# Reordering the projections of a one-core MLA + NSA transformer block: where the second projection and the branch values stand, which queue stores, and who makes low parts

## The chip, the cores and the metric

The kernel runs on one core of a Trainium2 chip. The metric is the device time of one execution in microseconds (us), taken as the median of several. The core has a matrix engine (PE), a vector engine (DVE), a scalar engine (ACT), GpSimd (POOL) and SyncE (SP); the last two issue transfers on DMA queues of their own. Each engine runs its own instructions strictly in the order written for it and waits on semaphores for the others.

## The reference

The block has a width of 1024, a sequence of 1024 tokens and one layer, and all in float32:

```python
h = h + token_mixer(rmsnorm(h, attn_norm), w_in, ...)
h = h + conv_ffn(h, ffn_norm, w_up, conv_w, conv_b, w_down)
return rmsnorm(h, final_norm)

def token_mixer(n, w_in, ...):
    z = n @ w_in        # c_q 384, c_kv 256, k_rope 32, q 512, six k/v of 128, 24 gates
    o_mla = mla_attention(c_q, c_kv, k_rope, ...)
    o_nsa = nsa_attention(q_n, k_c, v_c, k_s, v_s, k_w, v_w, gates, ...)
    return concatenate([o_mla, o_nsa], -1) @ w_o
```

`mla_attention` norms `c_q` and `c_kv`, projects them a second time (`rmsnorm(c_q) @ w_uq` gives the queries of 8 heads, `rmsnorm(c_kv) @ w_ukv` the keys and values), rotates the rope parts and does causal softmax attention. `nsa_attention` has 8 heads over 2 groups and three branches: a compressed one (`k_c`, `v_c` pass a small MLP by blocks of 32 tokens), a selected one (the top 16 of 16 blocks, so all causal keys) and a window of 512. Their outputs are summed under sigmoid gates. `conv_ffn` is a gated FFN of 2816 channels with a causal convolution of width 3.

## The kernel before, in words

**Precision.** A float32 operand is split into a high part (a rounded copy, made by ACT) and a low part (the operand minus its high part, made by DVE or POOL). A product takes three matmuls: high by high, high by low and low by high (`mm3`). A tile of a *Dense* item is 128 output channels by 1024 tokens, in a PSUM buffer `A` of two banks (there are two such buffers), with 8 steps over the input channels of 6 matmuls each. DVE then evacuates it in two instructions that also scale (`evac_scaled`, L212), and buffer `A` is free again.

**Stages.** In the profile of before: until 50 us the first three input tiles are computed while `x` streams in, with the norm of `x`. From 50 to about 206 us come the items of `run_items`: window keys (`kw`), gates and rope keys (`gr`), three tiles of `c_q`, four NSA query tiles (`q_tile`, stored to DRAM as `qnd`), the branch values (`Values`: 8 tiles of 128 tokens by 256 channels, 24 matmuls of 256 columns each, in PSUM buffer `B`, evacuated by ACT into `vsw`), and two tiles of `c_kv`. The second projection follows (206 to 266 us): six query tiles (`proj("q")`, 18 matmuls each; four of nope rows and two of rope rows, which `rotate` turns), then four key tiles (`proj("kv")`, 12 matmuls), each with two `mla_value` tiles behind it (6 matmuls each, buffer `B`, evacuated by ACT at L562). Each query or key tile is split (`split_rows`: high on ACT L428, low on DVE or POOL L429) and stored to DRAM as `qd` and `kd` (L568, L573). Then `attend(plan)` runs NSA query tiles 2 to 7, MLA pairs and the two short NSA tiles; the output projection, the FFN and the last norm come after it.

**What attention starts with.** NSA tile 2 takes its queries back from `qnd` (`fetch`, L727), splits them into `qs` (`prep`, L738 and L739), and multiplies them with `kd[j, g]`: the selected and window keys, loaded back from `kswd` into a doubled layout and split (`dup`, L591). Products go to PSUM buffer `A` (L629). DVE adds a mask (`dsel`, `dwin`) while taking a minimum (`soften`, L637), ACT takes the exponential (L640), PE transposes (L651), and PE multiplies by `vsw` (L666). The compressed branch goes its own way at the start of each NSA tile: PE L744 into `B`, DVE L746 and L749, POOL L750 and L751, ACT L755 (exponential), DVE L756.

**What sets the order.** The program is written as one sequence; each engine gets its instructions in that order, apart from local moves that a scheduler makes. `later(n, fn)` holds a step back until `tick()` has been called n times (after each step of a Dense item, for example). Transfers are issued by SP (`load`, `move`) or by POOL (`side`), in the order of that queue. Buffers come from rings: 37 of one size (`big`), 4 (`wide`), 3 for weights that are loaded (`w`). A buffer that is taken again makes its new writer wait for the last reader of the old content, a store included.

Of the kernel before, what the change touches and what calls it, by code (L numbers as in the profile page):

```python
# [17 lines left out]
P = 128  # L18
# [26 lines left out]
WARM = 8  # L45
FIRST = 1
RC, RR = (6, 0), (6, 2)
# [3 lines left out]
def body(ctx: ExitStack, tc: tile.TileContext, io, out):  # L51
# [57 lines left out]

    def split_g(x, g):  # L110

        hi, lo = big(list(x.shape), F32R, "hi"), big(list(x.shape), F32R, "lo")
# [117 lines left out]
    rs_x = big([P, T], name="rsx")  # L230
    first_w = [{} for _ in range(3)]


# [25 lines left out]
    def x_tile(k, s):  # L259
        n = s.stop - s.start  # L260
        x = big([P, n], name="x")
        in_turn(load, x, io["xT"][k * P:(k + 1) * P, s])

        def parts():
            h, l = split_g(x, col(C_AN + k))
# [62 lines left out]
    class Dense:  # L328
# [5 lines left out]
        def prep(self):  # L334
            self.w = split(load_w(self.ap, [P, KD, self.mw]), new=wide)

# [9 lines left out]
    def run_items(items, ahead=2):  # L346
        for j in range(min(ahead, len(items))):
            items[j].prep()
        for j, it in enumerate(items):
            it.run()  # L350
            if j + ahead < len(items):
                items[j + ahead].prep()

# [6 lines left out]
    def compress(src, pos0, w1n, w2n, put, t0):  # L360
        st = {}

        def gather():
            st["w1"] = [load_w(io[w1n][:, 8 * j:8 * j + 8], [P, 8, P]) for j in range(2)]
            st["w2"] = half([P, 64], name="w2")
# [50 lines left out]
    def rotate(t, n):  # L416

        w = big([P, T], name="sw")
        dve.stream_shuffle(out=w[:n], in_=t[:n], mask=[(j + 16) % 32 for j in range(32)])
        for c in range(2):  # L420
            s = slice(c * 512, (c + 1) * 512)
            pool.tensor_tensor(out=t[:n, s], in0=t[:n, s], in1=rope[0][c][:n], op=OP.mult)
            dve.tensor_tensor(out=w[:n, s], in0=w[:n, s], in1=rope[1][c][:n], op=OP.mult)
            pool.tensor_tensor(out=t[:n, s], in0=t[:n, s], in1=w[:n, s], op=OP.add)

    def split_rows(t, n, le="dve", new=wide):
        h, l = new([P, T], F32R, "hi"), new([P, T], F32R, "lo")
        act(h[:n], t[:n], AF.Copy)  # L428
        (dve if le == "dve" else pool).tensor_tensor(out=l[:n], in0=t[:n], in1=f(h)[:n], op=OP.subtract)  # L429
        return h, l  # L430

    def done_kw(o):
        t = evac_scaled(o, 1.0, rs_x)
        move(ksw_d[1], t)

    def done_gr(o):
# [16 lines left out]
        def rope_put():  # L453
            for j, t in enumerate(split_rows(kr, 32)):
                move(kr_d[j], f(t)[0:32])

        later(4, rope_k)

    lat = {n: dict(t=[], acc=big([P, T], name="acc"), rs=big([P, T], name="rs" + n)) for n in ("q", "kv")}

    def latent(n, m0, count, rank, gain):
        def done(o):
            L = lat[n]
            t = evac_scaled(o, 1.0, rs_x, name="c" + n)
            L["t"].append(t)
            sumsq(L["acc"], t, len(L["t"]) == 1)
            i = len(L["t"]) - 1
# [6 lines left out]
            if len(L["t"]) == count:  # L474
                later(6, lambda: L.update(rc=rms_cols([L["acc"]], rank)))
                later(9, lambda: rms_rows(L["rs"], L["rc"]))

        return [Dense(io["w_in"][m0 + i], done) for i in range(count)]

    def q_tile(r):  # L480
        def done(o):
            move(qn_d[:, r], evac_scaled(o, col(C_QS + r), rs_x))

        return Dense(io["w_in"][M_QN + r], done)

    vsw = [big([P, 4, 256], name="vsw") for _ in range(2)]

    class Values:


        def prep(self):
            self.w = [split(load_w(io["w_v"][:, 4 * j:4 * j + 4], [P, 4, 256])) for j in range(2)]

# [15 lines left out]
    def weights(n, ap, kt, w):  # L509
        def go(k):  # L510
            wts.setdefault(n, []).append(split(load_w(ap[k * P:(k + 1) * P], [P, w])))
        return [lambda k=k: go(k) for k in range(kt)]

    items = [Dense(io["w_in"][M_KW], done_kw), Dense(io["w_gr"], done_gr, 64)]
    items += latent("q", M_CQ, 3, RANK_Q, C_QN)
    items += [q_tile(r) for r in range(4)] + [Values()]
    items += latent("kv", M_CKV, 2, RANK_KV, C_KVN)
    for j, fn in enumerate(weights("q", io["w_uq"], 3, 768)):
        later(100 + 2 * j, fn)

# [12 lines left out]
    dist = {}  # L533
    later(50, masks)
    later(75, mask_sel)
    run_items(items)


# [11 lines left out]

    vm = [big([P, 2, 512], name="v") for _ in range(4)]

# [11 lines left out]

    def put_rows(t, dst, m, le, new=wide):
        for j, t in enumerate(split_rows(t, P, le, new)):
            for a in range(2):
                move(dst[2 * m + a, j, 0:64, :], f(t)[64 * a:64 * a + 64])  # L568

    def put_rope(t, m):  # L570
        for j, t in enumerate(split_rows(t, P)):
            for a in range(4):
                move(q_d[4 * m + a, j, 64:96, :], f(t)[32 * a:32 * a + 32])  # L573

    for j, fn in enumerate(weights("kv", io["w_ukv"], 2, 1024)):
        later(4 + 3 * j, fn)
    for m in range(4):
        t = proj("q", m, -MLA_SCALE)
        later(1, lambda t=t, m=m: put_rows(t, q_d, m, "pool" if m % 2 else "dve"))
    for m in range(2):  # L580
        t = proj("q", 4 + m, -MLA_SCALE)
        later(2, lambda t=t: rotate(t, P))
        later(9, lambda t=t, m=m: put_rope(t, m))

# [3 lines left out]
    def dup(j, g):  # L588
        t = sb.tile([P, T], F32, name=nm("kw"), tag="w", bufs=NW)
        for q in range(2):  # L590
            load(t[64 * q:64 * q + 64], ksw_d[j][64 * g:64 * g + 64])  # L591
        kd[j, g] = split(t)

    for j in range(2):
        for g in range(2):
            later(1 + 3 * g + 10 * j, lambda j=j, g=g: dup(j, g))

# [123 lines left out]
    def nsa_tile(i):  # L721
# [71 lines left out]
        def unit(br, rp):  # L793
            j = br - 1
            kb, d, v0 = (0, dist["sel"], 0) if br == 1 else (max(0, i - 4), dist["win"], 128)
            n = (i + 1 - kb) * P
            rows = []
            for g in range(2):
                for r in (2 * rp, 2 * rp + 1):
# [4 lines left out]

                    rows.append(dict(passes=passes, n=n, d=d[:, d.shape[1] - n:], scale=SLOPES[h], total=None, h=h))

# [9 lines left out]
            def totals():  # L816
                for row in rows:
                    c = 8 * br + row["h"]
                    row["total"] = st["tot"][:, c:c + 1]

            return u, [(-1, totals)]
# [137 lines left out]
    for m in range(4):  # L959
# [618 lines left out]
```

## Time and profile before

| | |
|---|---|
| time, median of 3 runs | 1411.15 us (1410.7 to 1412.43) |
| the profiled execution's own time | 1415.98 us |
| its span in the trace | 1414.2 us, 18969 instructions |
| mean granted TensorE clock | 0.981 |
| stages of the part that is changed | 0 to 50 first tiles; 50 to 206 first projection; 206 to 266 second projection; attention from there |

The page gives the busy share of each engine over the span and in 40 slices of 35.4 us. The slices that matter here are the first eight. A view of waits tells for an engine how long it stood still, at which of its lines, and which instruction of another engine ended that; in the timeline the same stands in brackets behind the instruction that waited. Times of matmuls overlap, so the distance from one start to the next is the pace.

### The profile page before, as it was taken

How to read it: one execution, taken by the hardware profiler on the slowest of the kernel's cores; microseconds unless marked ns; L12 is line 12 of the kernel's file. 1: busy time of each engine (PE TensorE's matmuls, PEld its weight loads, DVE VectorE, ACT ScalarE, POOL GpSimd, SP SyncE). 2: the span in 40 equal slices, each digit the busy share in tenths (PEclk: the TensorE clock that was granted, in tenths of full speed). 3: DMA queues.
4: the chain of work that ended last, by engine and by line, in shares of the span. 5: the costliest groups of instructions: out<-in, count | busy, mean ns of one | idle time of the engine just before them, and what ended most of it. 6: DMA issues, size and time to landing. Idle time of an engine off the chain costs nothing.

```text
span 1414.2 us, 18969 instructions
## 1 busy us (share of the span) xinstructions
PE 1354.6 (96%) x6996; PEld 1092.5 (77%) x6996; DVE 1016.3 (72%) x1587; ACT 669.6 (47%) x1213; POOL 469.3 (33%) x347
## 2 busy tenths in 40 slices
PE   8999999599999999999998999999999999999995
PEld 7788987467887767877877778888888888888785
DVE  6463017677776766685598997787787877998796
ACT  6022122576765656673345554444444445354371
POOL 4246525414333434420000025556665551000100
PEclk9999999799999999999999999999999999999998
DMA  6131314811112117643651131222212237754543
GB/s 223 60 128 60 116 45 127 219 46 42 39 50 79 42 50 188 193 150 129 225 192 53 65 119 70 75 90 89 82 67 75 90 126 245 278 184 135 155 135 120
DMA packets 69117, 164.58 MB, mean 116 GB/s; under 512 B 9288, under 2 KB 22744, under 8 KB 69024
## 3 DMA queue, kind: packets, MB, share of 16 engines
q1 hardware_dynamic: 60768, 145.53, 31.5%
q0 software_dynamic: 5376, 13.24, 3.3%
q10 hardware_dynamic: 2880, 4.60, 0.9%
q8 instruction: 55, 0.90, 0.3%
q14 instruction: 38, 0.31, 0.1%
HBM read 126.25 MB, written 37.09 MB: 115 GB/s over the span
## 4 chain that ended last, share of the span: by engine, by line
PE 54%; DVE 25%; ACT 7%; issue 5%; POOL 4%; DMA 3%; SPq 1%; DVEq 0%; ACTq 0%; POOLq 0%
PE A L629 6%; DVE wp L96 6%; PE O L666 6%; PE B L651 5%; PE A L204 4%; PE A L205 4%; PE A L207 4%; PE B L977 3%; PE B L979 3%; PE B L978 3%; PE A L977 3%; PE A L979 3%; PE A L978 3%; ACT hc L1051 3%; DVE hg L1163 3%
## 5 line engine op out<-in xcount | busy, mean ns | idle before, releaser
L640 ACT ACTIVATE p<-p,low 128x640 f32<-128x640 f32 (+7 forms) x192 | 142.6, 744 | 50.9 <-DVE low L637 47.3
L977 PE MATMUL B<-hi,wp 128*128 128x512 f32 x340 | 132.7, 390 | 0.9 <-DVE hg L1163 0.9
L978 PE MATMUL B<-lo,wp 128*128 128x512 f32 x340 | 132.6, 390 | 0.0
L98 POOL TENSOR_TENSOR wp<-w,wp 128x512 fp32r<-128x512 f32 x34 | 56.3, 1655 | 229.7 <-ACT wp L1112 229.7
L979 PE MATMUL B<-hi,wp 128*128 128x512 f32 x340 | 132.2, 389 | 0.0
L651 PE MATMUL B<-ident,p 128*128 128x128 f32 x816 | 123.1, 276 | 4.3 <-ACT pt L606 1.6
L651 PEld LDWEIGHTS B<-ident,p 128*128 128x128 f32 x816 | 96.7, 141 | 22.6 <-issue 6.2
L1112 ACT ACTIVATE wp<-ws 128x512 fp32r<-128x512 f32 x88 | 53.6, 628 | 99.8 <-DVE ws L1106 64.6
L96 DVE TENSOR_TENSOR wp<-ws,wp 128x512 fp32r<-128x512 f32 x54 | 66.9, 1243 | 44.6 <-ACT wp L1112 44.6
L204 PE MATMUL A<-hi,hi 128*128 128x512 f32 (+1 forms) x228 | 90.5, 397 | 1.0 <-DVE z L212 1.0
L205 PE MATMUL A<-lo,hi 128*128 128x512 f32 (+1 forms) x228 | 89.5, 393 | 0.0
L609 DVE COPY pt<-B 128x512 f32<-128x512 f32 (+3 forms) x154 | 77.5, 510 | 16.0 <-PE B L651 15.0
L606 ACT ACTIVATE pt<-B 128x512 f32<-128x512 f32 (+3 forms) x134 | 64.2, 481 | 50.6 <-PE B L651 50.2
L1051 ACT ACTIVATE hc<-hg,prm 128x1024 f32<-128x1024 f32 x44 | 54.5, 1243 | 66.3 <-DVE hg L1163 66.3
L104 ACT ACTIVATE hi<-w 128x1024 fp32r<-128x1024 f32 (+2 forms) x34 | 34.4, 1022 | 100.1 <-PE A L205 60.0
L1053 DVE SCALAR_TENSOR_TENSOR hc<-hg,prm,hc 128x1022 f32<-128x1022 f32 x44 | 78.1, 1776 | 0.6
L629 PE MATMUL A<-hi,qs 128*128 128x320 f32 (+5 forms) x192 | 64.8, 390 | 14.0 <-DVE pr L212 10.1
L977 PE MATMUL A<-nh,wp 128*128 128x512 f32 x188 | 74.4, 396 | 3.7 <-ACT q L1143 3.7
L666 PE MATMUL O<-pt,vsw 128*64 128x256 f32 x528 | 76.3, 387 | 0.1
L977 PEld LDWEIGHTS B<-hi,wp 128*128 128x128 f32 x340 | 64.0, 188 | 15.0 <-issue 1.3
L1052 DVE SCALAR_TENSOR_TENSOR hc<-hg,prm,hc 128x1023 f32<-128x1023 f32 x44 | 58.1, 1320 | 24.0 <-ACT hc L1051 23.9
L98 POOL TENSOR_TENSOR wp<-ws,wp 128x512 fp32r<-128x512 f32 x34 | 54.4, 1600 | 62.4 <-ACT wp L1112 60.5
(320 smaller groups left out, 3730.5 us busy)
## 6 DMA issues: line engine op xcount, KB each, us to landing
w<-in_w_up SPq DMA_DIRECT2D x50, 512.0 KB, 3.3
hidd<-hid SPq DMA_DIRECT2D x22, 512.0 KB, 2.6
w<-in_w_down SPq DMA_DIRECT2D x22, 512.0 KB, 3.4
a<-in_w_down SPq DMA_DIRECT2D x44, 256.0 KB, 4.4
b<-hidd SPq DMA_DIRECT2D x33, 256.0 KB, 5.2
w<-in_w_o SPq DMA_DIRECT2D x16, 512.0 KB, 3.3
x<-in_xT SPq DMA_DIRECT2D x15, 512.0 KB, 6.4
rb<-scr POOLq DMA_DIRECT2D x48, 128.0 KB, 2.9
```

Source lines behind the costliest of these rows:

```text
L96: dve.tensor_tensor(out=o, in0=a, in1=f(b), op=OP.subtract)
L98: pool.tensor_tensor(out=o, in0=a, in1=f(b), op=OP.subtract)
L204: mm(outs[c], wh, hs[c], start=start, stop=False)
L205: mm(outs[c], wh, ls[c], start=False, stop=False)
L629: mm(a[:, s, :w], lh, rh[:, s * w:(s + 1) * w], start=j == 0, stop=j == len(passes) - 1)
L640: act(p, p, AF.Exp, bias=low, scale=-1.0, accum_out=r["total"])
L651: nc.tensor.transpose(b[:, k * P:(k + 1) * P], self.rows[y]["p"][:, (4 * q + k) * P:(4 * q + k + 1) * P], ident)
L666: mm(o[64 * x:64 * x + 64, z * P:2 * P], self.value(x, k), self.pt[x, k // 4][:, k % 4, z:, :], start=k == 0, stop=k == last - 1, skip_gro ...
L977: mm(b, wh, h, start=start, stop=False, skip_group_check=skip)
L978: mm(b, wh, l, start=False, stop=False, skip_group_check=skip)
L979: mm(b, wl, h, start=False, stop=stop, skip_group_check=skip)
L1051: later(n, lambda: act(o, x, AF.Identity, bias=col(C_CB + m), scale=w[2]))
```

## The change

The change has four parts; the lines of the new file differ from the old by a few (products L629 are L632 there, `soften` L637 is L640, the evacuation L212 is L211, the low part of `split_rows` L429 is L440, `mla_value` L559 to L561 are L564 to L566, `Values` L500 to L502 are L514 to L516).

1. **Order.** The list of items is now `kw`, `gr`, three `c_q` tiles, NSA query tile 0, MLA query tiles 0 and 1, NSA query tile 1, MLA query tiles 2 and 3, NSA query tile 2, MLA (rope) query tiles 4 and 5, `c_kv` 0, `c_kv` 1, NSA query tile 3, and then `keys_and_values`: the four key tiles with their `mla_value` tiles, and `Values` last. The doubled keys (`dup`) and NSA tile 2's queries (`fetch_first`, `prep_first`) are put into `Values`.
2. **Stores.** All stores to `qnd`, `qd`, `kd`, `krd` and the second one to `kswd` are issued by POOL (`side`) instead of SP (`move`): 55 issues.
3. **Low parts.** Splits of weights and rows, the products and sums of `rotate` and the sums of squares of `c_q` and `c_kv` are made by DVE instead of POOL.
4. **Buffers and dues.** `vsw`, `vm`, `acc` and `rs` are taken when first used; the weights of the compression sit in `big` instead of `w`; rows of MLA queries are split into `big`, of MLA keys into `wide`; the two halves of the first tile of `x` share a buffer for each part; the norms of `c_q` and `c_kv` come after 4 and 7 ticks instead of 6 and 9.

```diff
     def split_rows(t, n, new=big):
         h, l = new([P, T], F32R, "hi"), new([P, T], F32R, "lo")
         act(h[:n], t[:n], AF.Copy)
-        (dve if le == "dve" else pool).tensor_tensor(out=l[:n], in0=t[:n], in1=f(h)[:n], op=OP.subtract)
+        dve.tensor_tensor(out=l[:n], in0=t[:n], in1=f(h)[:n], op=OP.subtract)
...
     def prep(self):
-            self.w = split(load_w(self.ap, [P, KD, self.mw]), new=wide)
+            self.w = split(load_w(self.ap, [P, KD, self.mw]), le="dve", new=wide)
...
-        for j, t in enumerate(split_rows(t, P, le, new)):
+        for j, t in enumerate(split_rows(t, P, new)):
             for a in range(2):
-                move(dst[2 * m + a, j, 0:64, :], f(t)[64 * a:64 * a + 64])
+                side(dst[2 * m + a, j, 0:64, :], f(t)[64 * a:64 * a + 64])
...
-    plan[0][0][1].pop(0)[1]()
-    first = plan[0][0][1].pop(0)[1]
-    for m in range(4):
-        t = proj("kv", m, 1.0)
-        later(1, lambda t=t, m=m: put_rows(t, k_d, m, "dve", big))
-        if m == FIRST:
-            first()
-        mla_value(2 * m)
-        mla_value(2 * m + 1)
+    fetch_first, prep_first = [plan[0][0][1].pop(0)[1] for _ in range(2)]
...
+    def keys_and_values():
+        vm.extend(big([P, 2, 512], name="v") for _ in range(4))
+        for m in range(4):
+            key(m)
+            mla_value(2 * m)
+            mla_value(2 * m + 1)
+            if m == 1:
+                values.prep()
+                mask_sel()
+        for n, fn in enumerate([lambda j=j, g=g: dup(j, g) for j in range(2) for g in range(2)]):
+            later(2 + 3 * n, fn)
+        later(1, fetch_first)
+        later(10, prep_first)
+        values.run()
...
+    items = [Dense(io["w_in"][M_KW], done_kw), Dense(io["w_gr"], done_gr, 64)] + cqs + [qs[0]]
+    items += queries(0, 1) + [qs[1]] + queries(2, 3) + [qs[2]] + queries(4, 5) + [ckvs[0], start_kv, ckvs[1], qs[3]]
+    items += [keys_and_values]
+    run_items(items)
```

The order of instructions shows the moves. The first place is PE where attention begins. In the kernel before, the products L629 follow straight on the last `mla_value` tile (`B_1949`; `hi_1738` and `lo_1739` are the first doubled keys, `qs_1822` NSA tile 2's split queries, L744 is the compressed branch's product):

```order
L560 MATMUL B_1949<-lo_1532,hi_1428 128x512
L561 MATMUL B_1949<-hi_1531,lo_1429 128x512
L559 MATMUL B_1949<-hi_1595,hi_1509 128x512
L560 MATMUL B_1949<-lo_1596,hi_1509 128x512
L561 MATMUL B_1949<-hi_1595,lo_1510 128x512
L629 MATMUL A_1957<-hi_1738,qs_1822 128x384
L629 MATMUL A_1957<-lo_1739,qs_1822 128x384
L744 MATMUL B_1971<-kcb,qn_1726 128x128 x4
L629 MATMUL A_1964<-hi_1738,qs_1822 128x384
```

In the changed kernel the last `mla_value` tile (`B_1700`) is followed by the 192 matmuls of `Values` (`B_1708` to `B_1929`), and the products, L632, follow on the last of those:

```order
L566 MATMUL B_1700<-hi_1394,lo_1442 128x512
L514 MATMUL B_1708<-hi_1611,hi_94 128x256
L515 MATMUL B_1708<-lo_1612,hi_94 128x256
L516 MATMUL B_1708<-hi_1611,lo_95 128x256
```

```order
L514 MATMUL B_1929<-hi_1617,hi_194 128x256
L515 MATMUL B_1929<-lo_1618,hi_194 128x256
L516 MATMUL B_1929<-hi_1617,lo_195 128x256
L632 MATMUL A_1955<-hi_1739,qs_1865 128x384
L632 MATMUL A_1955<-lo_1740,qs_1865 128x384
L632 MATMUL A_1962<-hi_1739,qs_1865 128x384
L632 MATMUL A_1962<-lo_1740,qs_1865 128x384
L747 MATMUL B_1969<-kcb,qn_1734 128x128 x4
```

The compressed product now also stands behind both first product tiles, where before it stood between them.

The second place is DVE at the same point. Before, the last key tile's evacuation (`pr_1930`) stands behind the compressed branch (`sc_1976`, `lowc_1978`, `tot_1818`) and behind the low part of key tile 2 (`lo_1895`):

```order
L212 SCALAR_TENSOR_TENSOR pr_1876<-A_1851,rskv_418 128x512 x2
L429 TENSOR_TENSOR lo_1859<-pr_1721,hi_1858 128x1024
L746 TENSOR_TENSOR sc_1976<-B_1971,dcmp 128x512
L749 TENSOR_REDUCE lowc_1978<-sc_1976 128x8
L756 TENSOR_REDUCE tot_1818<-sc_1976 128x4x2
L429 TENSOR_TENSOR lo_1895<-pr_1876,hi_1894 128x1024
L212 SCALAR_TENSOR_TENSOR pr_1930<-A_1910,rskv_418 128x512 x2
L739 TENSOR_TENSOR qs_2061<-w_2059,qs_2061 64x512
L429 TENSOR_TENSOR lo_1942<-pr_1930,hi_1941 128x1024
L637 ISA p_1960,low_1961<-A_1957,dsel_1195 128x384
```

In the changed kernel the last two key tiles' evacuations (`pr_1641`, `pr_1681`) come one after the other, with no row of the compressed branch before them, and all low parts of the doubled keys (`lo_1740` to `lo_1900`) and the first four tiles' `qs` stand before the first mask row of attention (L640):

```order
L211 SCALAR_TENSOR_TENSOR pr_1641<-A_1628,rskv_1349 128x512 x2
L211 SCALAR_TENSOR_TENSOR pr_1681<-A_1668,rskv_1349 128x512 x2
L440 TENSOR_TENSOR lo_1653<-pr_1641,hi_1652 128x1024
L440 TENSOR_TENSOR lo_1693<-pr_1681,hi_1692 128x1024
L95 TENSOR_TENSOR lo_1740<-kw_1736,hi_1739 128x1024
L95 TENSOR_TENSOR lo_1799<-kw_1795,hi_1798 128x1024
L742 TENSOR_TENSOR qs_1865<-qn_1734,qs_1865 64x512
L95 TENSOR_TENSOR lo_1832<-kw_1828,hi_1831 128x1024
L742 TENSOR_TENSOR qs_1865<-qn_1734,qs_1865 64x512
L742 TENSOR_TENSOR qs_2059<-w_2057,qs_2059 64x512 x2
L742 TENSOR_TENSOR qs_2351<-w_2349,qs_2351 64x512 x2
L95 TENSOR_TENSOR lo_1900<-kw_1896,hi_1899 128x1024
```

The third place is GpSimd's queue in the changed kernel between the last NSA query tile and attention: it issues the stores of the four key tiles, and the mask `dsel` stands between those of tiles 1 and 2 (before, this queue held none of these stores, and `dsel` was made during the first projection):

```order
L495 DMA qnd<-z_1521 128x1024
L573 DMA kd<-hi_1553 64x1024 x2
L573 DMA kd<-lo_1554 64x1024 x2
L573 DMA kd<-hi_1593 64x1024 x2
L573 DMA kd<-lo_1594 64x1024 x2
L217 IOTA dsel_1623 128x1024
L222 TENSOR_SCALAR m_1625<-dsel_1623 128x1024
L223 TENSOR_TENSOR dsel_1623<-dsel_1623,m_1625 128x1024
L573 DMA kd<-hi_1652 64x1024 x2
L573 DMA kd<-lo_1653 64x1024 x2
L573 DMA kd<-hi_1692 64x1024 x2
L573 DMA kd<-lo_1693 64x1024 x2
```

On SP's queue, the loads of `kw` (from `kswd`) and of NSA tile 2's queries no longer have any store of `qd` or `kd` ahead of them.

More of the change, by code (lines that the diff above doesn't have):

```diff
@@ L45 @@
 WARM = 8
-FIRST = 1
 RC, RR = (6, 0), (6, 2)
@@ L264, in parts @@
         def parts():
-            h, l = split_g(x, col(C_AN + k))
+            if n < T and not x0:
+                x0.extend(big([P, T], F32R, t) for t in ("hi", "lo"))
+            h, l = split_g(x, col(C_AN + k), [t[:, s] for t in x0] if n < T else None)
             for c in range(0, n, 512):
@@ L346, in run_items @@
     def run_items(items, ahead=2):
-        for j in range(min(ahead, len(items))):
-            items[j].prep()
-        for j, it in enumerate(items):
+        todo = [it for it in items if isinstance(it, Dense)]
+        for it in todo[:ahead]:
+            it.prep()
+        n = ahead
+        for it in items:
+            if not isinstance(it, Dense):
+                it()
+                continue
             it.run()
-            if j + ahead < len(items):
-                items[j + ahead].prep()
+            if n < len(todo):
+                todo[n].prep()
+            n += 1
     kcb = const([P, P], name="kcb")
@@ L363, in gather @@
         def gather():
-            st["w1"] = [load_w(io[w1n][:, 8 * j:8 * j + 8], [P, 8, P]) for j in range(2)]
+            st["w1"] = [big([P, 8, P], name="w1") for _ in range(2)]
+            for j in range(2):
+                load(st["w1"][j], io[w1n][:, 8 * j:8 * j + 8])
             st["w2"] = half([P, 64], name="w2")
@@ L481, in done @@
         def done(o):
-            move(qn_d[:, r], evac_scaled(o, col(C_QS + r), rs_x))
+            side(qn_d[:, r], evac_scaled(o, col(C_QS + r), rs_x))
         return Dense(io["w_in"][M_QN + r], done)
-    vsw = [big([P, 4, 256], name="vsw") for _ in range(2)]
+    vsw = []
     class Values:
         def prep(self):
-            self.w = [split(load_w(io["w_v"][:, 4 * j:4 * j + 4], [P, 4, 256])) for j in range(2)]
+            self.w = [split(load_w(io["w_v"][:, 4 * j:4 * j + 4], [P, 4, 256]), le="dve") for j in range(2)]
+            vsw.extend(big([P, 4, 256], name="vsw") for _ in range(2))
         def run(self):
@@ L510, in go @@
         def go(k):
-            wts.setdefault(n, []).append(split(load_w(ap[k * P:(k + 1) * P], [P, w])))
+            wts.setdefault(n, []).append(split(load_w(ap[k * P:(k + 1) * P], [P, w]), le="dve"))
         return [lambda k=k: go(k) for k in range(kt)]
[L514 to L519, printed above, removed]
     def masks():
@@ L533, in body @@
     dist = {}
-    later(50, masks)
-    later(75, mask_sel)
-    run_items(items)
+    later(56, masks)
     def proj(n, m, scale):
@@ L549, in proj @@
         return evac_scaled(o, scale, L["rs"], name="pr")
-    vm = [big([P, 2, 512], name="v") for _ in range(4)]
+    vm = []
     def mla_value(i):
@@ L572, in put_rope, with query, key @@
             for a in range(4):
-                move(q_d[4 * m + a, j, 64:96, :], f(t)[32 * a:32 * a + 32])
-    for j, fn in enumerate(weights("kv", io["w_ukv"], 2, 1024)):
-        later(4 + 3 * j, fn)
-    for m in range(4):
+                side(q_d[4 * m + a, j, 64:96, :], f(t)[32 * a:32 * a + 32])
+    def query(m):
         t = proj("q", m, -MLA_SCALE)
[L579 to L583, printed above, removed]
+        if m < 4:
+            later(1, lambda: put_rows(t, q_d, m))
+        else:
+            later(1, lambda: rotate(t, P))
+            later(4, lambda: put_rope(t, m - 4))
+    def key(m):
+        t = proj("kv", m, 1.0)
+        later(1, lambda: put_rows(t, k_d, m, wide))
     kd = {}
@@ L591, in dup @@
             load(t[64 * q:64 * q + 64], ksw_d[j][64 * g:64 * g + 64])
[L592 to L596, printed above, removed]
+        kd[j, g] = split(t, le="dve")
     used = {"act": 0.0, "dve": 0.0}
@@ L794, in unit @@
             j = br - 1
-            kb, d, v0 = (0, dist["sel"], 0) if br == 1 else (max(0, i - 4), dist["win"], 128)
+            kb, dn, v0 = (0, "sel", 0) if br == 1 else (max(0, i - 4), "win", 128)
             n = (i + 1 - kb) * P
@@ L803, in passes @@
                         return [(st["qs"][:, g, r], kd[j, g][p][:, kb * P:]) for p in range(2)]
-                    rows.append(dict(passes=passes, n=n, d=d[:, d.shape[1] - n:], scale=SLOPES[h], total=None, h=h))
+                    rows.append(dict(passes=passes, n=n, scale=SLOPES[h], h=h))
             def value(g, k):
```

42 lines of the change are left out of this document (28 added, 14 removed).

## The prediction, on record before the result

> **What bounds the kernel now.** I began with the page of the profile: the span, the busy share of each engine and the 40 slices (35.4 us each).
>
> ```profile
> span 1414.2 us, 18969 instructions
> PE 1354.6 (96%) x6996; PEld 1092.5 (77%) x6996; DVE 1016.3 (72%) x1587; ACT 669.6 (47%) x1213; POOL 469.3 (33%) x347
> PE   8999999599999999999998999999999999999995
> PEclk9999999799999999999999999999999999999998
> ```
>
> PE is busy for 96% of the span, so a change that doesn't take matmuls away can only win PE's idle time and the time at a reduced clock. One slice in the middle stands out: the eighth (248 to 283 us) has PE at 5 tenths and the clock at 7. It is the seam between the second projection and attention, which is where the change works. So the second view is PE's waits between 50 and 300 us (engine, line, instruction waited for: total us, times, longest):
>
> ```profile
> PE A L629 <- DVE pr L212: 10.1, 1, 10.1
> PE B L559 <- ACT v L562: 4.3, 1, 4.3
> PE A L629 <- DVE low L637: 2.4, 1, 2.4
> PE B L194 <- DVE rmr L184: 1.8, 1, 1.8
> ```
>
> These four lie in or next to the second projection, 10.06 + 4.29 + 2.39 + 1.84 = 18.6 us. The timeline of PE, DVE, ACT and POOL around the largest says why (start, us, engine, line; in brackets the idle time and what ended it):
>
> ```profile
> 262.82 0.39 PE L559 MATMUL B<-hi,hi 128*128 128x512 f32 x1
> 265.89 1.05 PE L744 MATMUL B<-kcb,qn 128*128 128x128 f32 x8
> 266.98 0.69 DVE L746 TENSOR_TENSOR sc<-B,dcmp 128x512 f32<-128x512 f32 x1 [4.77 <-PE B L744]
> 267.71 0.69 DVE L749 TENSOR_REDUCE lowc<-sc 128x8 f32<-128x512 f32 x1
> 268.47 1.04 POOL L750 TENSOR_TENSOR sc<-sc,lowc 128x512 f32<-128x512 f32 x1 [9.68 <-DVE lowc L749]
> 270.67 0.63 ACT L755 ACTIVATE sc<-sc 128x512 f32<-128x512 f32 x1 [8.77 <-POOL sc L751]
> 271.33 0.69 DVE L756 TENSOR_REDUCE tot<-sc 128x8 f32<-128x512 f32 x1 [2.94 <-ACT sc L755]
> 273.22 2.53 DVE L429 TENSOR_TENSOR lo<-pr,hi 128x1024 fp32r<-128x1024 f32 x1 [1.21 <-ACT hi L428]
> 275.68 1.27 DVE L212 SCALAR_TENSOR_TENSOR pr<-A,rskv 128x512 f32<-128x512 f32 x2
> 277.01 0.69 PE L629 MATMUL A<-hi,qs 128*128 128x384 f32 x1 [10.06 <-DVE pr L212]
> 278.55 1.22 DVE L429 TENSOR_TENSOR lo<-pr,hi 128x1024 fp32r<-128x1024 f32 x1
> ```
>
> PE is done with the last tiles at 266.94 and needs buffer `A` from the last key tile. That tile's evacuation (275.68) needs 1.27 us and has nothing to wait for by then; it stands on DVE behind `tot`, which comes back from a round trip over POOL and ACT, and behind a low part. The hole is thus a matter of queue order, not of work.
>
> The 4.29 us are the same thing one queue further on. ACT's evacuation of `mla_value` stood behind the high part of a doubled key, whose load SP had issued late, behind stores, as the chain of waits and PE's timeline show:
>
> ```profile
> 250.89 0.60 SPq L568
> 251.53 3.74 DMA kw<-kswd
> 255.29 1.06 ACT hi L104
> 256.98 0.75 PE L559 MATMUL B<-hi,hi 128*128 128x512 f32 x1 [4.29 <-ACT v L562]
> ```
>
> Each hole has a tail at a lower granted clock. The stretches behind them (window, length, busy time of PE, PEld, DVE, ACT, POOL, then clock, DMA share, GB/s):
>
> ```profile
> 224.20:226.70 2.50, 2.50 (x9) 2.04 (x9) 1.36 (x3) 0.72 (x1) 0.00 (x0) 0.57 0.20 72
> 256.90:260.50 3.60, 3.52 (x9) 2.80 (x9) 2.02 (x3) 2.72 (x5) 1.90 (x1) 0.53 0.59 171
> 277.00:281.00 4.00, 1.61 (x4) 1.13 (x5) 3.94 (x7) 2.35 (x5) 0.98 (x1) 0.50 0.89 223
> 281.00:285.00 4.00, 4.00 (x21) 3.81 (x19) 3.16 (x10) 2.37 (x8) 0.00 (x0) 0.58 0.89 266
> ```
>
> Busy time times what is missing of the clock: 2.50 x 0.43 = 1.1, 3.52 x 0.47 = 1.7, 1.61 x 0.50 = 0.8, 4.00 x 0.42 = 1.7.
>
> **The change part by part.** *Order.* `Values` keeps its 192 matmuls and goes behind the last key tile. Its length, from its first matmul to the first one behind it, is 183.92 - 160.88 = 23.0 us:
>
> ```profile
> 160.88 0.28 PE L500 MATMUL B<-hi,hi 128*128 128x256 f32 x1
> 183.92 0.40 PE L204 MATMUL A<-hi,hi 128*128 128x512 f32 x1
> ```
>
> PE computes these with buffers `B` and ACT evacuates them, so the last key tile's buffer `A` has 23 us and the two `mla_value` tiles' 2.7 to come free (12 matmuls at 0.227, since 12 of 512 and two of 384 columns lie between 262.82 and 265.89; 25.7 in all). What DVE has to do in that time: 1.27 for the evacuation, two low parts of rows at 1.22, four low parts of doubled keys at the same size, and eight small `qs` rows at about 0.69, together 1.27 + 2.44 + 4.88 + 5.5 = 14.1 us; if four of the low parts ran at 2.53, as the one above did while POOL was at work, 19.3. Both fit. The doubled keys' loads meet no stores on SP's queue any more. So the 10.06 and the 4.29 go. The 2.39 (masks behind `qs` and a low part at 278.55) go too, because those rows now stand ahead of the seam. The 1.84 is the chain of small DVE operations of a norm, which now falls behind `c_kv` 1 with NSA query tile 3 over it (48 matmuls, 10.9 us) instead of ahead of a projection. Gain of waits: **18.6 us**.
>
> With the holes go their tails: 1.1 + 1.7 + 0.8, of the last 1.7 half, since the first masks and exponentials also set the pace there, and 0.6 for the 16 small matmuls of the norm (2.43 us from 221.80 to 224.23, against 16/15 of 129.5 - 127.8 = 1.8):
>
> ```profile
> 221.80 2.78 PE L194 MATMUL B<-ident,rmr 128*128 128x128 f32 x16 [1.84 <-DVE rmr L184]
> 224.23 0.77 PE L204 MATMUL A<-hi,hi 128*128 128x512 f32 x1
> L194 PE MATMUL B<-ident,rmr x16: 271/275/275, 127.8 to 129.5; 128*128 128x128 f32 x16
> ```
>
> Together **5.0 us**; bounds 3.4 (nothing behind 277) and 5.9 (all of the 1.7).
>
> What is late next: the compressed branch. Its chain lay inside the 10 us hole; now PE runs into attention at full pace and the chain starts with it: 0.69 + 0.69 + 2 x 1.04 + 0.63 = 4.1 us, and ACT's table load of 1.28 can only come after the last `Values` tile's evacuation:
>
> ```profile
> 260.61 1.28 ACT L755 ACT_TABLE_LOAD   x1
> ```
>
> Bounds 0 (other rows fill it) and 5.4 (all of it on PE's path). I take **3.0**: 0.9 of the table load, since the first minimum is ready some 0.4 after it starts, and half of the chain.
>
> *Low parts.* The split groups of POOL and DVE between 50 and 281 us:
>
> ```profile
> L98 POOL TENSOR_TENSOR lo<-w,hi 128x1024 fp32r<-128x1024 f32 x13 | 33.0, 2550 | 41.9 <-ACT hi L104 29.8 <-DMA w<-in_cv_w 12.1
> L429 DVE TENSOR_TENSOR lo<-pr,hi 128x1024 fp32r<-128x1024 f32 x8 | 12.3, 1532 | 7.0 <-ACT hi L428 6.9
> 50.00:246.00 196.00, 193.30 (x1002) 162.85 (x1003) 80.90 (x100) 45.10 (x53) 97.37 (x48) 0.99 0.30 94
> ```
>
> What POOL makes in 2.55 us costs DVE 1.22 to 1.53. Of the 1024-wide size DVE takes over 13 + 4 doubled keys + 2 rows + 3 sums of squares = 22, that is 27 us; three of 768 (2.8) and eight half-size steps of `rotate` (5.5) make 35. DVE was busy for 80.9 of 196 us, so it becomes busy for about 116 of some 200: still no bound. Its cost is only in order: where a low part stands ahead of an evacuation. By the order I find one such place, the weights of NSA query tile 2 ahead of tile 1's evacuation; with POOL's masks beside it I take **0.4 us** (0 to 1.0, of the 1.3 that lie between 1.22 and 2.53). At the front, two low parts (1.22 + 0.6) enter the first norm's chain, and three more matmuls (at the half-pace distance of 0.43) stand ahead of a wait for the first weights: bounds -1.3 to +1.9, taken as nothing.
>
> *Stores.* 55 issues on GpSimd instead of SP, and their landing:
>
> ```profile
> L785 POOL DMA_DIRECT2D rb<-scr x48: 522/529/602, 313.5 to 572.2; - x48
> DMA to landing us min/median/max: 2.7/2.9/8.9
> kd<-hi SPq DMA_DIRECT2D x8, 256.0 KB, 3.2
> 165.25 3.63 POOL L223 TENSOR_SCALAR m<-dsel 128x1024 f32<-128x1024 f32 x1
> ```
>
> 55 x 0.53 = 29 us of GpSimd's time, which it has, as it gives up its low parts. From the first key tile to attention it has 16 issues (8.5 us) and the mask `dsel` (three operations, the longest 3.63, so under 11) in 40 us. Landing: 2.9 here, 3.2 on SP's queue; taken as equal. Parts 4's buffers add nothing by themselves.
>
> The sum against the profiled execution (1415.98): 18.6 + 5.0 - 3.0 - 0.4 = 20.2, giving 1395.8. That execution is 4.8 above the median of the runs; the holes are the same program in both, so I take the 20.2 off the median: 1411.15 - 20.2 = **1391.0 us**.
>
> **The rivals.** *R1, the hole comes back in part.* ACT's order puts evacuations of `Values` tiles behind the split of NSA tile 2's queries, whose buffer is free only when a store of key tile 2 has landed, and that store stands on GpSimd behind the mask `dsel` and earlier stores. For: the seam would wait for another queue, as it did before. Against: by the sums above the store goes out some 12 us ahead of its need. Price: the 10.06 come back, 20.2 - 10.1 = 10.1 gained, 1401 us. *R2, DVE is late throughout.* A tile's evacuation must be through when the next tile ends, 4.1 us (18 matmuls) behind a query tile. With two low parts of 2.53 ahead of it, it would be late by 2 x 2.53 + 1.27 - 4.1 = 2.2; at nine of the six query, four NSA query and four key tiles that is 20, and the gain is given back: about 1411, no change. For: DVE makes all low parts now. Against: it is at 58%, and 2.53 was seen beside POOL's low parts, which are gone. *R3, slower: the stores land late on GpSimd's queue.* Key tile 0's high part must have landed before key tile 2's takes its buffer, and this one before NSA tile 2's queries do: two landings in a row, of L each. PE's work ahead of the hole ended at 266.94, with 1.4 us of attention in it; less the 4.29 + 1.84 and their tails (3.4), attention's first product comes at about 256, `Values` at 233, the keys (96 matmuls) at 211, and key tile 0's store after 12 matmuls, evacuation, copy and issue at 216.5. 216.5 + L + 1.1 (copy) + 0.5 + L + 0.6 has to be under 244.5, when the fifth `Values` tile needs its PSUM buffer: L under 13. From there each microsecond costs two, and from L = 13 + 20.2/2 = 23 the change is slower; at L = 26, 1417 us. The row above has a longest landing of 8.9, which speaks against it.
>
> The Trainium skill speaks against part 2 here: its page "DMA: Bandwidth & Descriptors", section "Issuing engine by pattern", gives simple loads and stores to SyncE, as the generally faster path. No row here shows it (2.9 against 3.2). The Trainium skill, "SBUF — State Buffer", section "SBUF: two separate sides", tells of such a store of 620 ns that took 3100 beside a copy on DVE; five times 2.9 would be an estimated 14.5 us, past the point of 13 and short of 23, which would leave 1394.
>
> **How the numbers follow.** Forecast 0.74, R1 0.12, R2 0.08, R3 0.06. The forecast's own range goes from 18.6 + 5.9 + 1.3 - 0 = 25.8 (1385.4) to 18.6 + 3.4 - 5.4 - 1.0 - 1.9 = 13.7 (1397.5). With R1 the range is 1385 to 1401. A change under 0.2% (2.8 us) can't be told from none. Faster: 0.74 + 0.12 + 0.01 of R2 = 0.87; same 0.07; slower 0.06.
>
> **What would show it.** Right: PE's waits from 50 to 300 us without the first four, or with none over 2 us; a clock of 1.00 through the seam; the first product with `vsw` (L666), before at 285.91, at about 266. DVE's `lo` at 1.2, not 2.5. Wrong: a wait of PE in `Values` on ACT's `vsw` (R1 or R3, told apart by the landing of `kd` on GpSimd's queue, near 3 or over 13); waits of PE of 1 to 3 us at each query tile on DVE's `pr` (R2); or the holes gone and the end not earlier, which would mean that the slack stood elsewhere.

## The result and the profile after

The changed kernel takes **1388.44 us** (median of 4 runs, 1385.77 to 1389.71), beside 1411.79 for the kernel before: a ratio of 0.9828 with a 95% interval of 0.9815 to 0.9842. That is 23.35 us by the medians, 24.3 by the ratio (22.3 to 26.1). The forecast was 1391.0 in a range of 1385 to 1401, faster with a chance of 0.87. Timed again beside other kernels, it took 1387.03 beside 1413.64 (0.9819, 0.9797 to 0.9842).

The page of the profile after: span, busy shares and the two rows of slices. The eighth slice, which had 5 tenths for PE and 7 for the clock, is full.

```profile
span 1387.9 us, 18985 instructions
PE 1348.8 (97%) x6996; PEld 1088.5 (78%) x6996; DVE 1022.8 (74%) x1626; ACT 669.5 (48%) x1213; POOL 412.0 (30%) x363
PE   9999999999999999999998999999999999999996
PEclk9999999999999999999999999999999999999998
```

PE's waits between 50 and 300 us (engine, line, instruction waited for: total us, times, longest). All four rows of before are gone; what is left is small.

```profile
PE A L203 <- DVE z L211: 1.5, 1, 1.5
PE A L632 <- DVE low L640: 0.8, 2, 0.5
PE B L766 <- ACT sc L758: 0.8, 1, 0.8
PE B L772 <- ACT tc L609: 0.7, 1, 0.7
```

Not all of this is new. The wait at L772 (0.66, at 292.58) and one of the two at L632 (0.33, at 291.19) stand some 30 us behind the first product with `vsw`. In the kernel before the same two waits stand as far behind it, and so beyond 300 us, as its timeline shows:

```profile
315.88 0.50 PE L629 MATMUL A<-hi,qs 128*128 128x512 f32 x1 [0.33 <-DVE low L637]
317.27 1.12 PE L769 MATMUL B<-tc,vcb 128*128 128x512 f32 x2 [0.66 <-ACT tc L606]
```

So the new waits at the seam are the other one at L632 (0.46) and that at L766 (0.76), 1.2 us in all.

The stages (window, length, busy time of PE, PEld, DVE, ACT, POOL, then clock, DMA share, GB/s). From 50 to 256 us PE never stops, and the clock stays at 1.00 through the start of attention.

```profile
50.00:206.00 156.00, 156.00 (x748) 127.98 (x749) 88.27 (x126) 38.94 (x42) 43.23 (x52) 1.00 0.38 121
206.00:256.00 50.00, 50.00 (x325) 45.88 (x324) 26.50 (x33) 23.57 (x35) 16.13 (x20) 1.00 0.52 148
256.00:262.00 6.00, 4.64 (x30) 3.42 (x28) 5.00 (x16) 4.92 (x13) 2.08 (x2) 1.00 0.01 1
262.00:270.00 8.00, 8.00 (x47) 5.19 (x47) 5.97 (x19) 6.28 (x19) 0.00 (x0) 1.00 0.00 0
```

PE's timeline where `Values` (L516) ends and attention (L632) begins:

```profile
254.47 0.28 PE L516 MATMUL B<-hi,lo 128*128 128x256 f32 x1
254.59 0.34 PE L632 MATMUL A<-hi,qs 128*128 128x384 f32 x1
261.18 0.66 PE L766 MATMUL B<-ident,sc 128*128 128x128 f32 x4 [0.76 <-ACT sc L758]
262.09 0.65 PE L669 MATMUL O<-pt,vsw 128*64 128x256 f32 x2
```

The first product of attention comes at 254.59 instead of 265.55, the first with `vsw` at 262.09 instead of 285.91. Of the 26.3 us between the two spans (1414.2 and 1387.9), 23.8 thus lie ahead of this point, 0.95 of them ahead of the first Dense item (it starts at 49.91 instead of 50.86).

### The profile page after: what moved, and what is told of

Its sections match the earlier page's. It is cut to its first block, busy times and chain, and to the rows that moved or that the text cites. A ratio compares the mean times of both kernels' runs of the same rounds, so it can differ in the third digit from the quotient of the medians.

```text
span 1387.9 us, 18985 instructions
## 1 busy us (share of the span) xinstructions
PE 1348.8 (97%) x6996; PEld 1088.5 (78%) x6996; DVE 1022.8 (74%) x1626; ACT 669.5 (48%) x1213; POOL 412.0 (30%) x363
## 4 chain that ended last, share of the span: by engine, by line
PE 59%; DVE 23%; ACT 7%; issue 4%; POOL 4%; DMA 1%; DVEq 0%; ACTq 0%; POOLq 0%
PE A L632 8%; PE O L669 8%; DVE wp L95 7%; PE B L654 6%; PE A L203 4%; PE A L204 4%; PE A L206 4%; PE B L1006 3%; PE B L1008 3%; PE B L1007 3%; PE A L1006 3%; PE A L1008 3%; ACT hc L1080 3%; PE A L1007 3%; DVE hg L1192 3%
## 5 line engine op out<-in xcount | busy, mean ns | idle before, releaser
L1006 PEld LDWEIGHTS B<-hi,wp 128*128 128x128 f32 x340 | 64.0, 188 | 14.9 <-issue 1.3
L1007 PEld LDWEIGHTS B<-lo,wp 128*128 128x128 f32 x340 | 64.0, 188 | 13.3 <-DVE lo L95 0.2
L1008 PEld LDWEIGHTS B<-hi,wp 128*128 128x128 f32 x340 | 63.9, 188 | 13.3
```

The costliest lines, as they stand in the source:

```text
L1006: mm(b, wh, h, start=start, stop=False, skip_group_check=skip)
L1007: mm(b, wh, l, start=False, stop=False, skip_group_check=skip)
L1008: mm(b, wl, h, start=False, stop=stop, skip_group_check=skip)
```

## The experiments

Each kernel was timed beside the kernel before. Gains are worked out as (1 - ratio) x 1411.8 us, with the interval of the ratio.

| kernel | order and buffers (1, 4) | stores on GpSimd (2) | low parts on DVE (3) | median us | ratio, interval | gain us |
|---|---|---|---|---|---|---|
| changed | new | yes | yes | 1388.44 | 0.9828, 0.9815 to 0.9842 | 24.3 |
| stores_on_sp | new | no | yes | 1390.65 | 0.9850, 0.9833 to 0.9866 | 21.2 |
| lows_on_pool | new | yes | no | 1386.48 | 0.9817, 0.9803 to 0.9832 | 25.8 |
| order_alone | new | no | no | 1397.87 | 0.9905, 0.9880 to 0.9929 | 13.4 |
| before_stores_and_lows | old | yes | yes | 1398.14 | 0.9895, 0.9873 to 0.9918 | 14.8 |
| before_stores_on_pool | old | yes | no | 1409.62 | 0.9990, 0.9977 to 1.0002 | 1.4 |
| before_lows_on_dve | old | no | yes | 1409.95 | 0.9992, 0.9979 to 1.0004 | 1.1 |

Part 4 was not taken away by itself: what the buffers and dues do is contained in every row called new.

### Taking parts away from the changed kernel

*Stores back on SyncE* (the same in all five places where `side` had replaced `move`):

```diff
-                side(dst[2 * m + a, j, 0:64, :], f(t)[64 * a:64 * a + 64])
+                move(dst[2 * m + a, j, 0:64, :], f(t)[64 * a:64 * a + 64])
```

> The changed kernel with its 55 stores issued by SyncE again; order, low parts and buffers as changed. Theory A (the new order alone took the holes away, because 23 us of Values now cover the seam): the loads of the doubled keys stand behind stores again, but have more than 20 us of cover, so the time stays within 2 us of the changed kernel, 1386 to 1391. Theory B (the loads behind the stores on SyncE's queue were what opened the holes): at least the 4.3 us of the evacuation of mla_value come back, 1393 or more.

Measured 1390.65 (1389.89 to 1391.36), which is inside theory A's range. Its interval overlaps that of the changed kernel, so the 3 us between the two gains are not settled. The transfers' rows (queue, count, size, median us to landing) show that the key stores land sooner from SyncE's queue. First this kernel:

```profile
kd<-hi SPq DMA_DIRECT2D x8, 256.0 KB, 3.0
kd<-lo SPq DMA_DIRECT2D x8, 256.0 KB, 3.5
```

and the changed one:

```profile
kd<-hi POOLq DMA_DIRECT2D x8, 256.0 KB, 3.9
kd<-lo POOLq DMA_DIRECT2D x8, 256.0 KB, 4.8
```

*Low parts back on GpSimd* (also in `Values`, the second projection's weights, `rotate` and the sums of squares; the rows of query tiles 1 and 3, which GpSimd split in the kernel before, stay on DVE):

```diff
-            self.w = split(load_w(self.ap, [P, KD, self.mw]), le="dve", new=wide)
+            self.w = split(load_w(self.ap, [P, KD, self.mw]), new=wide)
...
-        kd[j, g] = split(t, le="dve")
+        kd[j, g] = split(t)
```

> The changed kernel with its low parts, rotation and sums of squares of the first and second projection on GpSimd again; order and stores as changed. Theory A (order): GpSimd gets some 60 us of work back and its 29 us of issues, which it has room for in 200 us; some evacuations and stores come later, 0 to 4 us lost, 1388 to 1393. Theory C (the holes went because DVE and GpSimd no longer slow each other, and because low parts are shorter on DVE): half of the gain or more is given back, 1400 or more.

Measured 1386.48 (1384.51 to 1387.77): nothing is lost. No worth of part 3 can be told once the order is new and the stores have left SyncE. Theory C falls.

*Both back: the order alone.*

> The changed kernel with both the stores on SyncE and the low parts on GpSimd, as before: only the order and the buffers are changed. Theory A: 1388 to 1394, four fifths of the gain or more. Theories B or C: 1400 or more.

Measured 1397.87 (1395.13 to 1403.6), between the two theories: a little over half of the gain. So either of parts 2 and 3 brings the rest or most of it, but one of them is needed. The three largest rows of PE's waits of this kernel between 50 and 300 us, and the chain that ends one of them (start, us, what):

```profile
PE A L632 <- DVE low L640: 3.1, 4, 1.4
PE B L173 <- POOL acc L162: 1.4, 2, 1.2
PE B L514 <- ACT v L567: 1.4, 1, 1.4
```

```profile
227.16 2.39 POOL lo L97
229.55 0.95 POOL dsel L217
230.58 4.03 POOL m L222
234.69 2.39 POOL dsel L223
237.11 0.70 ACT v L567
237.85 0.39 PE B L514
```

GpSimd makes low parts and the mask `dsel` one after the other, ACT's evacuation of an `mla_value` tile waits for the mask's end, and PE waits for that (1.35 us). This is one part of the loss. Counted from the first Dense item, the first product with `vsw` comes 8.2 us later than in the changed kernel (220.4 instead of 212.2 us). PE's waits up to there are 5.1 us longer: 1.4 for a norm's sum on GpSimd, this 1.35, and most of the rest for masks. Behind the longer of the norm's waits (1.22 us), 3.6 us run at a clock of 0.53, an estimated 1.7 us more. The remaining 1.4 us were not traced.

*`Values` ahead of the key tiles*, so that these stand directly ahead of attention again (`dup` and the queries' preparation then fall into the key tiles, the mask stands ahead of `Values`, and the weights of `Values` are prepared ahead of NSA query tile 3, a line that is not shown):

```diff
         vm.extend(big([P, 2, 512], name="v") for _ in range(4))
-        for m in range(4):
-            key(m)
-            mla_value(2 * m)
-            mla_value(2 * m + 1)
-            if m == 1:
-                values.prep()
-                mask_sel()
+        mask_sel()
+        values.run()
...
         later(1, fetch_first)
         later(10, prep_first)
-        values.run()
+        for m in range(4):
+            key(m)
+            mla_value(2 * m)
+            mla_value(2 * m + 1)
```

> The changed kernel with Values run ahead of the four key tiles instead of behind them; the key tiles stand directly ahead of attention again, stores and low parts as changed. Theory A (Values is the cover): a hole opens again where attention starts, between 2 us (the last evacuation of 1.3 and a low part of 1.2 ahead of it) and 8 us, with its tail at a reduced clock: 1391 to 1399. Theories B and C: no hole, within 2 us of the changed kernel.

Measured 1392.35 (1391.8 to 1394.1), ratio 0.9862 (0.9848 to 0.9877), whose interval doesn't touch that of the changed kernel: 4.8 us are given back, as theory A said. But the hole is not the old one: PE waits for the compressed branch, and a tail at half clock follows. A row of its waits:

```profile
PE B L766 <- ACT sc L758: 2.5, 1, 2.5
```

and two of its windows:

```profile
262.00:266.60 4.60, 1.51 (x6) 0.87 (x6) 3.39 (x8) 4.51 (x12) 0.00 (x0) 0.83 0.02 8
266.60:270.00 3.40, 3.40 (x16) 2.68 (x18) 2.42 (x7) 1.59 (x3) 0.00 (x0) 0.50 0.00 0
```

The place of `Values` is thus worth about a fifth of the gain when parts 2 and 3 are there.

### Adding parts to the kernel before

*The compressed branch moved away from the last evacuation.*

```diff
-        us[0][1].append((1, cmp_scores))
+        us[0][1].append((1 + 5 * (i == 2), cmp_scores))
```

`cmp_exp`, `cmp_turn` and `cmp_values` move by the same five steps.

> The kernel before with one thing moved: the compressed branch of NSA tile 2 comes five steps of attention later, so that DVE's three rows of it no longer stand ahead of the last key tile's evacuation. The prediction's reading (the 10.06 us hole is DVE's queue order alone): the evacuation then waits only for a low part ahead of it, the hole shrinks to 2 to 4 us, 1403 to 1406. Rival (behind that wait the next one ends only a little earlier: the high parts of doubled keys, whose loads SyncE issued behind stores, keep ACT and so the low part back): the hole keeps 7 us or more, 1408 to 1412.

Measured 1411.32 beside 1411.31, ratio 0.9996 (0.9982 to 1.0010): nothing. The prediction's reading of the 10 us hole falls. The rows it had pointed at are gone from the place, and the hole is as long as it was; the wait,

```profile
PE A L629 <- DVE pr L212: 10.7, 1, 10.7
```

and the rows of ACT and DVE that end it:

```profile
270.03 1.06 ACT L104 ACTIVATE hi<-kw 128x1024 fp32r<-128x1024 f32 x1 [10.13 <-DMA kw<-kswd]
272.06 2.54 DVE L429 TENSOR_TENSOR lo<-pr,hi 128x1024 fp32r<-128x1024 f32 x1 [10.59 <-ACT hi L428]
```

ACT stands for 10 us at the high part of a doubled key, whose load SyncE issued behind stores; the high part of key tile 2 stands behind it on ACT, its low part waits on DVE, and the last evacuation stands behind that.

*Part 2 alone: stores on GpSimd.* (The diff is that of `stores_on_sp`, turned round.)

> The kernel before with part 2 alone: the 55 stores on GpSimd's queue. The prediction's reading: the 4.29 us of mla_value go, since the doubled keys' loads come earlier, and DVE's queue order keeps the larger hole: 3 to 6 us gained, 1406 to 1409. Rival (stores on SyncE ahead of loads are the root of both holes): 10 us or more gained, 1401 or less. On GpSimd the stores stand in order with low parts of 2.55 us, so a loss is possible too: 1412 or more.

Measured 1409.62, ratio 0.9990 (0.9977 to 1.0002): no change that can be told. The load is early now, the 4.3 us of `mla_value` shrink to 2.2, and the hole grows to 16.7. The wait,

```profile
PE A L629 <- DVE pr L212: 16.7, 1, 16.7
```

and four rows from the end of the chain behind it (between the last three stand GpSimd's queue and a row of the compressed branch):

```profile
257.47 5.21 DMA kd<-lo
264.07 0.66 POOL lo L98
267.36 2.80 DMA kd<-hi
270.16 2.28 DVE qs L739
```

GpSimd's queue holds key stores behind low parts; queries (`qs`) wait on DVE for a store's landing, and the last evacuation stands behind `qs`.

*Part 3 alone: low parts on DVE.* (The diff is that of `lows_on_pool`, turned round; the rows of query tiles 1 and 3 go to DVE as well.)

> The kernel before with part 3 alone: low parts, rotation and sums of squares on DVE. The prediction's reading: DVE's queue at the seam gets longer by four low parts and the rotation, while each is shorter and the 1.84 us of the norm go: within 3 us of before, 1408 to 1414. Rival (low parts of 2.55 us on GpSimd, for which stores and behind them loads on SyncE wait, are what opens the holes): 7 us or more gained, 1404 or less.

Measured 1409.95, ratio 0.9992 (0.9979 to 1.0004): no change either. The 4.3 and the 1.8 us go, and the hole is 14.4 us:

```profile
PE A L629 <- DVE pr L212: 14.4, 1, 14.4
```

at the end of the same chain as in `before_cmp_later`:

```profile
259.99 4.41 DMA kw<-kswd
264.42 1.07 ACT hi L104
265.51 1.06 DVE lo L96
```

*Parts 2 and 3 together.*

> The kernel before with parts 2 and 3 together, order and buffers as before. Alone, part 2 measured 0.9990 and part 3 0.9992 of the time before. Theory A (at the old seam PE has too little work to cover the making of attention's inputs, and whatever queue is freed, another ends the hole): 0 to 6 us gained, 1405 to 1411, and a hole of 8 us or more stays in the trace ahead of the products. Rival (the two parts hold each other back, stores behind low parts on GpSimd, and only together they show): 10 us or more gained, 1401 or less.

Measured 1398.14, ratio 0.9895 (0.9873 to 0.9918): 14.8 us, against theory A and for its rival. The two parts hold each other back: with stores on SyncE the loads stand behind them; with stores on GpSimd they stand behind low parts, unless these have left too. The wait for the last evacuation is down to 1.8 us; what remains is the compressed branch, masks, and the clock:

```profile
PE B L763 <- ACT sc L755: 3.3, 1, 3.3
PE A L629 <- DVE low L637: 2.9, 3, 2.3
PE A L629 <- DVE pr L212: 1.8, 1, 1.8
```

and the stage as a window:

```profile
256.00:270.00 14.00, 8.01 (x29) 5.54 (x29) 11.60 (x28) 12.04 (x26) 6.96 (x12) 0.76 0.68 239
```

The new order takes this remainder (14.8 to 24.3). With `values_before_keys` at 19.5, about half of that belongs to the place of `Values`; for the rest of the order the two intervals just overlap, so its share is not settled.

### Sizes of single terms

*The compressed branch of tile 2 inside `Values`.*

```diff
+    early = [f for d, f in plan[0][0][1] if d in (1, 4)]
+    plan[0][0][1][:] = [e for e in plan[0][0][1] if e[0] not in (1, 4)]
...
         later(10, prep_first)
+        later(12, early[0])
+        later(15, early[1])
```

> The changed kernel with the compressed branch of NSA tile 2 (product, DVE, GpSimd, exponential with its table load) put into the last Values tiles. The prediction priced its exposure at the seam at 3.0 us (0 to 5.4); the trace after shows some 2.2 us of waits of PE there. Theory: these go, 1.5 to 2.5 us gained, 1386 to 1387. Rival: other rows of DVE and ACT take their place at the seam, within 0.5 us of the changed kernel.

Three executions took 1386.88, 1389.28 and 1390.06; a fourth, the profiled one, took 3003 us and is not counted. The ratio is 0.9845 (0.9825 to 0.9865): no gain. The expectation was too high from the start, as the waits at the seam that are new are 1.2 us, not 2.2. Whether other rows took the branch's place stayed open. The same edit was also made on the kernel with low parts on GpSimd, beside the changed kernel on the same chip:

> The changed kernel with its low parts on GpSimd again (1386.5 in an earlier run) and, besides, the compressed branch of NSA tile 2 put into the last Values tiles. If part 3 is worth nothing once the stores have left SyncE, and the compressed branch's exposure is of 1 to 2 us: 1384 to 1387, 1.5 us or more under the changed kernel. If part 3 does save time and the earlier result was its spread: 1388 or more.

> The changed kernel itself, on the chip and beside the runs of the next kernels, so that differences under 1% can be read: 1386 to 1391.

Measured 1385.84 (ratio 0.9813, 0.9790 to 0.9837) beside 1387.03 for the changed kernel: 1.2 us under it by the medians, with intervals that overlap almost wholly. This does not answer the question either. The trace of `lows_on_pool`, without the edit, has no wait for the branch (L766) to take away; its only wait at the seam is one of 0.46 us for a mask. With the edit, waits for masks are longer:

```profile
PE A L632 <- DVE low L640: 1.6, 2, 1.3
```

It is the lowest median measured, and not one that can be told from the changed kernel.

*Key stores twice.*

```diff
                 side(dst[2 * m + a, j, 0:64, :], f(t)[64 * a:64 * a + 64])
+                if dst is k_d:
+                    side(dst[2 * m + a, j, 0:64, :], f(t)[64 * a:64 * a + 64])
```

> The changed kernel with each of the 16 stores of MLA keys issued twice, one straight after the other, on GpSimd's queue: 16 x 0.53 = 8.5 us more of issues between the first key tile and attention, and the stores' buffers free later. The prediction gave these stores some 12 us of slack: if so, within 1.5 us of the changed kernel. Rival (the chain over GpSimd's stores and its mask is close to the path, R1): 4 us or more lost, 1392 or more, with PE waiting in Values or at the first products.

Measured 1397.99, ratio 0.9897 (0.9871 to 0.9923): 11 us lost against the changed kernel beside it (0.9819). The load was larger than planned, because the second store of a pair, which writes the same place, waited for the first to land. GpSimd stood still for 23.1 us at these stores (13.4 for low parts, 9.7 for high parts). PE's wait:

```profile
PE B L514 <- ACT v L567: 8.5, 1, 8.5
```

and the rows of GpSimd and ACT that lead from one to the other:

```profile
240.07 2.34 POOL L223 TENSOR_TENSOR dsel<-dsel,m 128x1024 f32<-128x1024 f32 x1
242.44 0.69 ACT L567 ACTIVATE v<-B,rmr 128x512 f32<-128x512 f32 x1 [14.44 <-POOL dsel L223]
```

In the changed kernel the mask's last row ends at 231.1 (its start 228.65 and 2.40); here at 242.4. So 11.4 us of lateness on GpSimd became 8.5 of waiting on PE and a tail at half clock (0.50 from 243.1 to 248.0). Both kernels start the first Dense item at 49.9, so the mask had an estimated 11.4 - 8.5 = 2.9 us to spare in the changed kernel. It is the same path as in `order_alone`. As the load was not the 8.5 us of the expectation and PE waited on the mask, not on the stores, the slack of the stores themselves was not measured; what is shown is that GpSimd's queue at this place is close to the path. It need not be: in `lows_on_pool` the same evacuation starts at 230.13 while the mask runs until 235.27. Which wait between the two engines makes this difference was not traced.

## Why the prediction was right, and where its steps were not

The time, the sign and the mechanism's outcome (holes and clock tails gone, little put in their place) came as forecast. Step by step:

- **Waits, 18.6 us.** All four rows are gone. Right in size. The first product with `vsw` came at 262.09, where about 266 was forecast.
- **Tails, 5.0.** The clock is 1.00 in every window from 50 to 270 us, so all of 1.1 + 1.7 + 0.8 + 1.7 + 0.6 = 5.9 went; the half of the 1.7 that was left to masks and exponentials was too careful. That the 1.84 us wait had a tail to lose belongs to the kernel before: the same wait in `before_stores_on_pool`, 1.89 us, had none.
- **Compressed branch, -3.0.** PE's two new waits there are 0.46 + 0.76 = 1.2 us, and taking the branch away brought nothing measurable. The term was more than twice too large.
- **Low part ahead of an evacuation, -0.4.** No such wait is in the trace.
- **Front, 0.** The added low parts show, since the wait for `z` at 50 us is 1.5 instead of 1.0 (1.5 in every trace with low parts on DVE, 1.0 in every other). The first Dense item starts at 49.91 instead of 50.86; but it starts at 48.29 in the second trace of the changed kernel itself, so this can't be put down to an edit.
- **Sum.** 18.6 + 5.9 - 1.2 = 23.3, beside 23.35 by the medians and 22.9 in the traces between the first Dense item and the first product with `vsw`; the forecast was 20.2.

Three statements on the way to the sum were wrong:

- **"The hole is thus a matter of queue order, not of work"**, with DVE's rows of the compressed branch as its cause. `before_cmp_later` takes these away and the hole stays at 10.7 us. Behind the wait that ended last stood another that ended hardly earlier: loads behind stores on SyncE, through ACT and a low part. The row in brackets names the last releaser, not what the time would be without it.
- **The gain was booked wholly to the order** ("So the 10.06 and the 4.29 go", since `Values` covers them; that the doubled keys' loads meet no stores any more is named there, but has no price of its own). The order alone brings 13.4 us; parts 2 and 3 alone bring 14.8; all together 24.3. `Values` behind the keys is worth 4.8 when the others are there. The forecast was right because the change had two remedies for one hole, and the sum had only to know that it closes. For this step that was luck: the order alone took 1397.87, just outside the forecast's own range of 1385.4 to 1397.5.
- **Parts 2 and 3 at nothing.** Neither shows alone in the old order (1.4 and 1.1, both within their intervals of none). On top of the new order one of them is worth some 8 to 12 us, and the second nothing that can be told from the runs. The low parts' price was right: 1217 and 1224 ns in these groups of the changed kernel, against 2550 on GpSimd.

```profile
L95 DVE TENSOR_TENSOR lo<-w,hi 128x1024 fp32r<-128x1024 f32 x13 | 15.7, 1217 | 9.2 <-ACT hi L103 9.2
L95 DVE TENSOR_TENSOR lo<-kw,hi 128x1024 fp32r<-128x1024 f32 x4 | 4.8, 1224 | 3.0 <-ACT hi L103 3.0
```

The rivals: R1 did not happen in the changed kernel, but its place, the mask and the stores on GpSimd's queue, is real: it cost 1.4 us in `order_alone` and 8.5 in `key_stores_twice`. It held `mla_value`'s evacuation, not the queries' split, and its margin in the changed kernel is an estimated 2.9 us, beside the 12 that the prediction gave to the store of key tile 2. R2 did not happen: DVE is busy for 88.27 of 156 us (57%, forecast 58) and PE never waits for it at a query tile. R3 did not happen: the key stores land after 3.9 and 4.8 us at the median, later than the 3.2 they were taken to equal, and the longest after 6.6, under 13.

The Trainium skill's rule that simple stores are generally faster from SyncE ("DMA: Bandwidth & Descriptors", section "Issuing engine by pattern") holds here for one transfer: 3.0 and 3.5 us against 3.9 and 4.8. It does not show in the time of the kernel, which was 1390.65 with SyncE's stores and 1388.44 with GpSimd's, with intervals of the ratios that overlap. Why the sooner landing brought nothing was not taken apart.

## What to carry to other kernels

A large wait in a trace tells where time is lost, and its releaser tells only who came last: before naming a cause, ask what would have ended the wait next, and take that one away too. In-order queues can hold the same hole open from several sides, so that each remedy alone shows nothing (0.9990 and 0.9992) and two together show 15 us; an edit that measured as nothing may be needed by the next. Work that needs nothing new (`Values` here) can be kept for the seam where everything else has to be made ready; here that was worth 4.8 us.

## What the runs showed of the hardware that was not expected

- A short wait can cost a tail at about half clock, and the length of the wait alone did not decide it. Ahead of the same 16 small matmuls of a norm PE waited 1.84 us in the kernel before and in `before_cmp_later`, and the 2.5 us behind these matmuls had a clock of 0.57 and 0.53; in `before_stores_on_pool` it waited 1.89 us there and the clock stayed at 1.00. After 2.46 us in `values_before_keys`, 266.6 to 270.0 had 0.50; after 2.25 us in `before_stores_on_pool` it was 1.00. In `order_alone` a wait of 1.22 us, ahead of 16 matmuls of one column, was followed by 0.53; after its 1.35 us wait and the 1.47 us one of the changed kernel the clock was 1.00. The Trainium skill ("TensorE: Matmul & The Clock Gate", section "Part 1: The HAM clock gate (the "warmup" mystery)") puts the return to half speed after an idle window of about 3.4 us. Each of these waits alone was under 3.4; in the longer stretch around the 2.46 us one, 262.0 to 266.6, PE was busy for 1.51 of 4.60 us. What decides between the two outcomes stays open here.
- The same 256 KB store took 3.9 to 4.8 us to land from GpSimd's queue and 3.0 to 3.5 from SyncE's, in otherwise equal kernels (medians). Other transfers that were under way at the time differ between the two, so this is not the price of the queue alone.

The windows of the first point that are not shown above, behind the 1.89 us of `before_stores_on_pool` and behind the 1.22 us of `order_alone`:

```profile
221.00:223.50 2.50, 2.50 (x13) 2.04 (x12) 1.70 (x3) 0.72 (x1) 0.00 (x0) 1.00 0.89 272
203.50:207.10 3.60, 3.60 (x10) 2.85 (x9) 0.60 (x7) 0.00 (x0) 0.00 (x0) 0.53 0.00 0
```
